# Values of four recurrent heads in one projection, and attention one head ahead, in a hybrid decoder layer

## The chip, the core and the metric

The kernel runs on one core of a Trainium2 chip, as one program. The core has a matrix engine (TensorE, "PE" in the profile, with its weight loads as "PEld"), a vector engine (VectorE, DVE), a scalar engine (ScalarE, ACT), a general engine (GpSimd, POOL) and an engine that here issues most transfers (SyncE, SP). Matrix products are accumulated in eight PSUM banks of 128 x 512 float32; everything else on the chip lies in SBUF. The metric is the device time of one execution in microseconds (us); lower is better. The median of 3 runs before the change is 2198.31 us (2196.97 to 2198.78).

## What is computed

One decoder layer over 2048 positions of width 1024, in float32. The part that the change touches is the mixer:

```python
u = rmsnorm(h, norm_mix_w[l])
proj = u @ w_in[l]                       # q, f, values, gate of 4 recurrent heads of 128; q, k, v of attention
f = lb + (1.0 - lb) * jax.nn.sigmoid(hf) # the decay of each key channel
# per head: S_t = diag(f_t) S_{t-1} + (1 - f_t) v_t^T,  o_t = S_t^T q_t   (in chunks)
o_hg = rmsnorm(o_hg, hg_norm_w[l]) * jax.nn.silu(hg)
# 8 query heads of 64 over 2 key heads, window of 128, a learned sink logit in each softmax
mix = jnp.concatenate([o_hg, o_att], axis=-1)
h = h + mix @ w_out[l]
```

After it come a gated MLP of width 2816 with a causal depthwise convolution, and a final rmsnorm. The change leaves those alone.

## The kernel before

The sequence is worked in two halves of 1024 positions, one after the other, and each half in three stages: the mixer, the output projection with the MLP's first two products (`out_proj`, `gate_up`), and the MLP's last product (`down`). A product in float32 is split: each operand is a high part and a low part, and three matmuls (high x high, high x low, low x high) stand for one. `prep` (L185) loads a weight block of 128 x 1024, lets ACT make the high part (L190) and DVE the low part (L191). `unit` (L194) is one projection to 128 output rows for 1024 positions: 8 blocks of the inner dimension x 3 x 2 halves = 48 matmuls of 512 columns, into two banks of the pool "mm", which has four.

The mixer runs over four recurrent heads, `h` = 0 to 3. `hgrn` is a Python generator, cut by `yield` into steps, and does for one head:

- projection f, then projection q ("hq" in the profile), then products of both (`Q` and `K`, one buffer each);
- a diagonal product ("pdiag", L544), then seven levels, m = 1, 2, 4, ... 64 (from L590 on). Each level is a matmul of `K` with `Q` ("plev", L569, L602 or L607), after which DVE multiplies `Q` (L609), `K` (L610) and `f` (L616), and the result is copied under a mask into the score matrix `ST`. The next level's matmul needs the new `Q` and `K`. In heads 0 to 2 levels below 32 take half as many matmuls, over a packed copy of `K` made by ACT (L566), with a small transfer to shift rows (L579). The last head takes 16 matmul instructions a level there (L602) and neither copy nor transfer;
- transposes of `K` ("pkn"), state updates ("pu", L647, then DVE L651), the gate's projection ("g"; in the last head it comes before the levels), the outputs ("po", L665 and L666, squared by ACT L667), their norm, transposes ("pot") and the gated result.

`attend` is a second generator, one call for two query heads (a "pair", `j` = 0 to 3): a projection ("q", scaled by DVE L435), scores ("psc", L459) with softmax on DVE and ACT, then in two steps transposes ("ppt"), masks (L498) and outputs ("poT", L506). Its banks are the two of the pool "at". In the last pair (`j` = 3) the outputs are split into high and low parts straight from the bank (L516, L517).

The loop over heads (from L1195 on) draws the steps of both generators in turn; pair `h` is drawn in head `h`. `project_v` (L688) makes the values of two heads at a time, in head 0 and in head 2: 8 blocks of positions x 8 x 3 = 192 matmuls of 256 columns, from two weight blocks in the ring "hi"/"lo", which has two of each. The bank is scaled into the values by ACT (L702), two copies of 128 x 128 each time.

The order in which the loop draws the steps is not the order on the engines. A planner simulates the program when it is built and fixes each engine's queue: what comes earlier in the program goes first, but work that waits is overtaken by later work that is ready, so far as its buffers are free. So a later unit's matmuls fill the time in which a level waits for DVE.

In the last head the mixed rows are split for the output projection (`split`, L223 and L224) into the buffers of `X`, which come free as the gate's projection has read them. `out_proj` then works in the order of blocks 0, 4, 1, 5, 2, 6, 7, 3, where block `h` is recurrent head `h` and block 4 + `j` is pair `j`. Its first three units ("pop") can begin before the mixer has ended. The table `BEHIND` holds the second one behind the first level of the last head, and parts of the third one behind "pu", "po" and "pot".

The pool "m" has eight buffers of 128 x 1024 for what lives across heads: each recurrent head's q and gate, each pair's q and output, and before the mixer the rows of x (first half) or of h (second half).

Of the kernel before, what the change touches and what calls it, by code (L numbers as in the profile page):

```python
# [8 lines left out]
F32 = mybir.dt.float32  # L9
# [30 lines left out]
NEG = -1.0e30  # L40
UT = 7
RAW = 3
VB = 2
KB = 2
WARM = 12
TAIL_WARM = 7
# [4 lines left out]
def hymba_layer(ctx: ExitStack, tc: tile.TileContext, a: dict, out: bass.AP):  # L51
# [378 lines left out]
    def attend(hf, j, X, invb, KS, V, mix, p):  # L430

        o = unit(a["w_att"][j], X, "q")
        qT = slot(f"att{j}")
        for b, bs in halves():
            nc.vector.scalar_tensor_tensor(qT[:, bs], o[b], 0.125, invb[:, bs], op0=ALU.mult, op1=ALU.mult)  # L435
            nc.scalar.activation(qT[:, bs], qT[:, bs], AF.Identity, bias=C.bq[:, j:j + 1])
        yield
        scs = []
        for g in range(NB):
            sc = p.tile([P, 2, 4, P], F32, tag="sc", name="sc", bufs=2)  # L440
            gs = slice(g * 512, (g + 1) * 512)
            for kv in range(2):
                r, other = rows(kv), rows(1 - kv)

                qh, ql = [p.tile([P, 512], F32R, tag="pp", name=n, bufs=4) for n in ("qh", "ql")]
                nc.scalar.copy(qh[r], qT[r, gs])
                nc.scalar.copy(qh[other], qT[r, gs])
                nc.vector.tensor_tensor(ql[r], qT[r, gs], qh[r].bitcast(F32), op=ALU.subtract)
                nc.scalar.copy(ql[other], ql[r].bitcast(F32))
                for i0 in (0, 2):  # L450
                    pb = ps("at", "psc")
                    first = hf == 0 and g == 0 and i0 == 0
                    for i in range(2):
                        n = g * 4 + i0 + i
                        w0 = 1 if first and i == 0 else 0
                        o = pb[:, i * 256 + w0 * P:(i + 1) * 256]
                        ks = slice((n + w0) * P, (n + 2) * P)
                        for t, qx in enumerate((qh, ql)):
                            nc.tensor.matmul(o, qx[:, (i0 + i) * P:(i0 + i + 1) * P], KS[:, kv, ks],  # L459
                                             start=t == 0, stop=t == 1)  # L460
                    pv = pb.rearrange("p (i w k) -> p i w k", i=2, w=2)
                    dst = sc[:, kv, i0:i0 + 2]
                    if first:
                        nc.vector.memset(dst[:, 0], NEG)
                        nc.scalar.copy(dst[:, 1], pv[:, 1, 0])
                    else:
                        nc.scalar.copy(dst, pv[:, :, 0])
                    nc.vector.copy_predicated(
                        dst, C.own.bitcast(U32).unsqueeze(1).to_broadcast([P, 2, P]), pv[:, :, 1])
            m = p.tile([P, 2, 4], F32, tag="mx", name="m", bufs=2)  # L470
            nc.vector.tensor_reduce(m.rearrange("p a b -> p (a b)"),
                                    sc.rearrange("p a b c -> p (a b) c"), axis=AX.X, op=ALU.max)
            sk = C.sinkb[:, j].unsqueeze(2).to_broadcast([P, 2, 4])
            nc.vector.tensor_tensor(m, m, sk, op=ALU.max)
            es = p.tile([P, 2, 4], F32, tag="es", name="es", bufs=2)
            nc.vector.tensor_tensor(es, sk, m, op=ALU.subtract)
            nc.vector.tensor_scalar(m, m, -1.0, None, op0=ALU.mult)
            den = p.tile([P, 2, 4], F32, tag="den", name="den", bufs=2)
            for kv in range(2):
                for i in range(4):  # L480
                    nc.scalar.activation(sc[:, kv, i], sc[:, kv, i], AF.Exp, bias=m[:, kv, i:i + 1],
                                         accum_out=den[:, kv, i:i + 1])
            nc.scalar.activation(es, es, AF.Exp)
            nc.vector.tensor_tensor(den, den, es, op=ALU.add)
            nc.vector.reciprocal(den, den)
            nc.vector.tensor_tensor(sc, sc, den.unsqueeze(3).to_broadcast([P, 2, 4, P]), op=ALU.mult)
            scs.append(sc)
        yield
        for g, sc in enumerate(scs):
            pm = []  # L490
            for kv in range(2):
                pm.append([p.tile([P, 4, P], F32, tag="pp", name=n, bufs=4) for n in ("po", "pp")])
                pt = ps("at", "ppt")
                for i in range(4):
                    nc.tensor.transpose(pt[:, i * P:(i + 1) * P], sc[:, kv, i], ident)
                ptv = pt.rearrange("p (i q) -> p i q", i=4)
                for dst, mk in zip(pm[kv], (C.ownT, C.prevT)):
                    nc.vector.tensor_tensor(dst, ptv, mk.unsqueeze(1).to_broadcast([P, 4, P]), op=ALU.mult)  # L498
            oT = ps("at", "poT")
            for i in range(4):  # L500
                n = g * 4 + i
                noprev = hf == 0 and n == 0
                for prev in range(1 if noprev else 2):
                    for kv in range(2):
                        r = rows(kv)
                        nc.tensor.matmul(oT[r, i * P:(i + 1) * P], V[:, n + 1 - prev, r], pm[kv][prev][:, i],  # L506
                                         start=prev == 0, stop=noprev or prev == 1)
            gs = slice(g * 512, (g + 1) * 512)
            if j < ATT_J - 1:
                nc.scalar.copy(qT[:, gs], oT)  # L510
                mix[4 + j] = qT
            else:
                if g == 0:
                    mix[4 + j] = new_x()
                h, l = mix[4 + j]
                nc.scalar.copy(h[:, gs], oT)  # L516
                nc.vector.tensor_tensor(l[:, gs], oT, h[:, gs].bitcast(F32), op=ALU.subtract)  # L517
            yield

    def hgrn(hf, h, X, invb, vs, WG, mix, p, fu=None):  # L520
# [166 lines left out]

    def project_v(hf, parts, X, rs, p):  # L688

        v = [p.tile([P, TT, P], F32, tag="v", name="v", bufs=VB) for _ in range(2)]  # L690
        for tt in range(TT):
            o = ps("mm", "pvv")
            t = slice(tt * P, (tt + 1) * P)
            for kt in range(KT):
                hi, lo = parts[kt // 4]
                xh, xl = X[kt]
                c = slice((kt % 4) * 256, (kt % 4 + 1) * 256)
                nc.tensor.matmul(o[:, 0:256], xh[:, t], hi[:, c], start=kt == 0, stop=False)  # L698
                nc.tensor.matmul(o[:, 0:256], xl[:, t], hi[:, c], start=False, stop=False)  # L699
                nc.tensor.matmul(o[:, 0:256], xh[:, t], lo[:, c], start=False, stop=kt == KT - 1)  # L700
            for i in range(2):
                nc.scalar.activation(v[i][:, tt], o[:, i * P:(i + 1) * P], AF.Identity, scale=rs[:, tt:tt + 1])  # L702
        return v

    def split_into(h, l, src, eng=None):
        return (nc.scalar.copy(h, src),  # L706
# [480 lines left out]
    for hf in range(NH):  # L1187
        X, kv, invb, rs, f0 = nxt
        with ExitStack() as st:
# [2 lines left out]
            mix = [None] * KT  # L1192
            vs = []
            M, WG = {}, {}
            for h in range(HG):  # L1195
                hg = hgrn(hf, h, X, invb, vs, WG, mix, p, f0 if h == 0 else None)
                at = attend(hf, h, X, invb, KS, V, mix, p)
                with tc.issue_after(summed.ins) if hf + h == 0 else ExitStack():
                    next(hg)
                if h == HG - 1:  # L1200
                    next(at)
                    next(hg)
                    for kt in (0, 4, 1, 5, 2, 6):
                        M[kt] = split(mix[kt])
                    next(hg)
                elif h % 2 == 0:
                    next(at)
                    wv = [prep(a["w_v"][h // 2, s]) for s in range(2)]
                    next(hg)
                    vs += project_v(hf, wv, X, rs, p)  # L1210
                else:
                    next(hg)
                    next(at)
                if h < HG - 1:
                    WG[h] = prep(a["w_g"][h])
                next(at)
                next(hg)
                if h < HG - 1:
                    next(hg)
                next(at)  # L1220
                if h < HG - 1:
                    next(at)
                    next(hg)
                else:
                    next(hg)
                    next(at)
            M[7], M[3] = mix[7], mix[3]
        with ExitStack() as st:
            p = pool(f"ffn{hf}", stack=st, reuse_waits="tile")
            kept, ops, hs, first, last = out_proj(hf, M, p)  # L1230
# [4 lines left out]
def _layout(i):  # L1235
# [14 lines left out]
    rows = [ar(P) + h * P for h in range(4)]  # L1250
    rows += [512 + np.concatenate([j * HD + ar(HD), (j + 4) * HD + ar(HD)]) for j in range(4)]
    w_out = i["w_out"][0][np.concatenate(rows)]
    w_v = np.stack([cols(w_in, 1024 + pr * 256 + ar(256)).reshape(P, 2, D).transpose(1, 0, 2) for pr in range(2)])
    conv = np.concatenate([i["conv_w"][0], i["conv_b"]], 0)
    d = {
        "xT": x.T.reshape(KT, P, S),
# [37 lines left out]
```

## Time and profile before

| What | Value |
|---|---|
| Time, median of 3 runs | 2198.31 us (2196.97 to 2198.78) |
| The profiled execution: span, first to last instruction | 2198.0 us |
| Mean granted TensorE clock | 0.997 |
| PE busy | 2180.4 us, 99% |
| DVE busy | 1639.5 us, 75% |
| ACT busy | 1049.9 us, 48% |
| Moved by DMA | 257.91 MB |
| Mixer, first half | about 45 to 400 us |
| Mixer, second half | about 1125 to 1490 us |

Matmuls overlap: a matmul of 512 columns is shown with some 390 ns, but the next one starts earlier, so "busy" is not a count of work done. The time from one matmul's start to the next one's is what a matmul costs in a row of them. The chain of waits shows that: there a piece is a run of instructions, with its start, the time that it took on the chain, and their count. In the lists of groups and of instructions the brackets at the end give the idle time of the engine ahead, and what ended it. The profile gives the span; the time that lies around it is not shown apart, and the median of the runs is 0.3 us above the span.

### The profile page before, as it was taken

How to read it: one execution, taken by the hardware profiler on the slowest of the kernel's cores; microseconds unless marked ns; L12 is line 12 of the kernel's file. 1: busy time of each engine (PE TensorE's matmuls, PEld its weight loads, DVE VectorE, ACT ScalarE, POOL GpSimd, SP SyncE). 2: the span in 40 equal slices, each digit the busy share in tenths (PEclk: the TensorE clock that was granted, in tenths of full speed). 3: DMA queues.
4: the chain of work that ended last, by engine and by line, in shares of the span. 5: the costliest groups of instructions: out<-in, count | busy, mean ns of one | idle time of the engine just before them, and what ended most of it. 6: DMA issues, size and time to landing. Idle time of an engine off the chain costs nothing.

```text
span 2198.0 us, 29524 instructions
## 1 busy us (share of the span) xinstructions
PE 2180.4 (99%) x11424; PEld 1834.0 (83%) x11424; DVE 1639.5 (75%) x2451; ACT 1049.9 (48%) x1848; POOL 6.3 (0%) x28
## 2 busy tenths in 40 slices
PE   9999999999999999999999999999999999999998
PEld 7988988888888888888889889888888888888888
DVE  6567568688887888885855666677888878887766
ACT  6445544454444445335735455544644444443353
POOL 1000000000000000000000000000000000000000
PEclk9999999999999999999999999999999999999999
DMA  4101112323333234964631111114132323259643
GB/s 155 51 32 48 39 41 68 119 74 102 104 109 108 89 127 143 372 241 156 209 125 41 44 36 51 58 39 134 58 125 92 125 91 109 98 183 393 233 144 130
DMA packets 94358, 257.91 MB, mean 117 GB/s; under 512 B 11594, under 2 KB 17546, under 8 KB 94218
## 3 DMA queue, kind: packets, MB, share of 16 engines
q1 hardware_dynamic: 88992, 251.30, 33.9%
q10 hardware_dynamic: 5226, 4.73, 0.7%
q8 instruction: 89, 1.46, 0.3%
q14 instruction: 51, 0.42, 0.1%
HBM read 195.10 MB, written 57.15 MB: 115 GB/s over the span
## 4 chain that ended last, share of the span: by engine, by line
PE 95%; DVE 3%; ACT 1%; DMA 1%; issue 0%; SPq 0%; DVEq 0%; ACTq 0%
PE X L877 7%; PE X L878 7%; PE X L879 7%; PE pop L212 7%; PE hq L212 4%; PE q L212 4%; PE f L212 4%; PE g L212 4%; PE Y L879 4%; PE Y L878 4%; PE Y L877 4%; PE pdx L1088 3%; PE pdx L1089 3%; PE pdx L1090 3%; PE pdy L1089 3%; PE pdy L1088 3%
## 5 line engine op out<-in xcount | busy, mean ns | idle before, releaser
L706 ACT CAST whi<-raw 128x1024 fp32r<-128x1024 f32 x88 | 92.6, 1053 | 109.2 <-PE X L878 68.2
L877 PE MATMUL X<-T,whi 128*128 128x512 f32 x352 | 136.9, 389 | 0.0
L878 PE MATMUL X<-T,whi 128*128 128x512 f32 x352 | 136.9, 389 | 0.0
L879 PE MATMUL X<-T,wlo 128*128 128x512 f32 x352 | 136.9, 389 | 0.0
L972 DVE SCALAR_TENSOR_TENSOR y<-ga,cw,y 128x1024 f32<-128x1024 f32 x88 | 112.5, 1281 | 26.0 <-ACT y L970 26.0
L884 ACT COPY u<-X 128x512 f32<-128x512 f32 x88 | 51.4, 585 | 133.3 <-PE X L879 133.1
L707 DVE TENSOR_TENSOR wlo<-raw,whi 128x1024 fp32r<-128x1024 f32 x88 | 107.3, 1220 | 0.0
L190 ACT CAST whi<-raw 128x1024 fp32r<-128x1024 f32 x57 | 59.5, 1048 | 93.1 <-PE q L212 31.9
L707 DVE TENSOR_TENSOR xld<-raw,xhd 128x1024 fp32r<-128x1024 f32 x72 | 80.8, 1133 | 19.1 <-ACT xhd L706 18.9
L706 ACT CAST xhd<-raw 128x1024 fp32r<-128x1024 f32 x72 | 69.7, 978 | 43.6 <-DMA raw<-act0T 14.8
L212 PE MATMUL pop<-XL,whi 128*128 128x512 f32 x256 | 86.1, 396 | 2.1 <-DVE XL L224 2.1
L212 PE MATMUL pop<-XH,wlo 128*128 128x512 f32 x256 | 85.2, 393 | 0.8 <-DVE wlo L191 0.8
L212 PE MATMUL pop<-XH,whi 128*128 128x512 f32 x256 | 84.5, 397 | 0.2
L878 PEld LDWEIGHTS X<-T,whi 128*128 128x128 f32 x352 | 66.1, 188 | 13.7
L877 PEld LDWEIGHTS X<-T,whi 128*128 128x128 f32 x352 | 66.1, 188 | 13.7
L879 PEld LDWEIGHTS X<-T,wlo 128*128 128x128 f32 x352 | 66.1, 188 | 13.7
L1088 PE MATMUL pdx<-xhd,hid 128*128 128x512 f32 x192 | 74.4, 391 | 1.0 <-ACT hid L706 1.0
L1089 PE MATMUL pdx<-xld,hid 128*128 128x512 f32 x192 | 74.7, 389 | 0.0
L1090 PE MATMUL pdx<-xhd,lod 128*128 128x512 f32 x192 | 73.7, 389 | 0.0
L698 PE MATMUL pvv<-whi,XH 128*128 128x256 f32 x256 | 73.5, 288 | 0.0
L191 DVE TENSOR_TENSOR wlo<-raw,whi 128x1024 fp32r<-128x1024 f32 x57 | 69.5, 1222 | 4.2 <-ACT whi L190 4.1
L699 PE MATMUL pvv<-whi,XL 128*128 128x256 f32 x256 | 72.6, 284 | 0.0
(379 smaller groups left out, 6563.3 us busy)
## 6 DMA issues: line engine op xcount, KB each, us to landing
wr<-in_w_down SPq DMA_DIRECT2D x90, 512.0 KB, 4.8
raw<-in_w_gate SPq DMA_DIRECT2D x44, 512.0 KB, 3.6
raw<-in_w_up SPq DMA_DIRECT2D x44, 512.0 KB, 3.6
raw<-act0T SPq DMA_DIRECT2D x20, 512.0 KB, 6.1
raw<-act1T SPq DMA_DIRECT2D x20, 512.0 KB, 10.1
act0B<-y SPq DMA_DIRECT2D x33, 256.0 KB, 2.6
act1B<-y SPq DMA_DIRECT2D x33, 256.0 KB, 2.4
raw<-in_w_out SPq DMA_DIRECT2D x16, 512.0 KB, 4.7
```

What stands on the lines that cost most here:

```text
L212: marks["unit"] = nc.tensor.matmul(o[b], w, x[:, bs], start=f, stop=l)
L698: nc.tensor.matmul(o[:, 0:256], xh[:, t], hi[:, c], start=kt == 0, stop=False)
L699: nc.tensor.matmul(o[:, 0:256], xl[:, t], hi[:, c], start=False, stop=False)
L706: return (nc.scalar.copy(h, src), (eng or nc.vector).tensor_tensor(l, src, h.bitcast(F32), op=ALU.subtract))
L707: (eng or nc.vector).tensor_tensor(l, src, h.bitcast(F32), op=ALU.subtract))
L877: nc.tensor.matmul(o, wh[:, ws], xh, start=i == 0 and not more, stop=False, skip_group_check=more)
L878: nc.tensor.matmul(o, wh[:, ws], xl, start=False, stop=False, skip_group_check=more)
L879: r = nc.tensor.matmul(o, wl[:, ws], xh, start=False, stop=i == 3, skip_group_check=more)
L972: nc.vector.scalar_tensor_tensor(y, g[:, w:w + HALF], C.cw[:, ft, w:w + 1], y, op0=ALU.mult, op1=ALU.add)
L1088: nc.tensor.matmul(o, wh[:, i, c], ah[:, i, cols], start=f, stop=False, skip_group_check=more)
L1089: nc.tensor.matmul(o, wh[:, i, c], al[:, i, cols], start=False, stop=False, skip_group_check=more)
L1090: nc.tensor.matmul(o, wl[:, i, c], ah[:, i, cols], start=False, stop=l, skip_group_check=more)
```

## The change

`project_v` is called once, in head 0, for all four heads. It takes four weight blocks (each for two of the eight inner blocks), two of them in the ring and two in the pool "m", and issues matmuls of 512 columns. Its bank is scaled by one ACT instruction of 128 x 512 into one tile for the values of all heads. The pool for values of two heads at a time goes.

The generators of all four pairs are made ahead of the loop. Head 0 draws pair 0 and pair 1, head 1 draws pair 2 (its projection after the levels, in the program's order), head 2 draws pair 3, and head 3 none. In head 3 seven blocks are split ahead of the levels, where there were six; the last pair's outputs are copied like the others' and split later. The host lays the weights out in four blocks of four heads. The scratch that the build sets aside for descriptors of another kind of DMA is made smaller.

```diff
-            if j < ATT_J - 1:
-                nc.scalar.copy(qT[:, gs], oT)
-                mix[4 + j] = qT
-            else:
-                if g == 0:
-                    mix[4 + j] = new_x()
-                h, l = mix[4 + j]
-                nc.scalar.copy(h[:, gs], oT)
-                nc.vector.tensor_tensor(l[:, gs], oT, h[:, gs].bitcast(F32), op=ALU.subtract)
+            nc.scalar.copy(qT[:, gs], oT)
+            mix[4 + j] = qT
...
-        v = [p.tile([P, TT, P], F32, tag="v", name="v", bufs=VB) for _ in range(2)]
+        v = p.tile([P, HG, TT, P], F32, name="v")
...
-                hi, lo = parts[kt // 4]
+                hi, lo = parts[kt // 2]
                 xh, xl = X[kt]
-                c = slice((kt % 4) * 256, (kt % 4 + 1) * 256)
-                nc.tensor.matmul(o[:, 0:256], xh[:, t], hi[:, c], start=kt == 0, stop=False)
-                nc.tensor.matmul(o[:, 0:256], xl[:, t], hi[:, c], start=False, stop=False)
-                nc.tensor.matmul(o[:, 0:256], xh[:, t], lo[:, c], start=False, stop=kt == KT - 1)
-            for i in range(2):
-                nc.scalar.activation(v[i][:, tt], o[:, i * P:(i + 1) * P], AF.Identity, scale=rs[:, tt:tt + 1])
-        return v
+                c = slice((kt % 2) * 512, (kt % 2 + 1) * 512)
+                nc.tensor.matmul(o, xh[:, t], hi[:, c], start=kt == 0, stop=False)
+                nc.tensor.matmul(o, xl[:, t], hi[:, c], start=False, stop=False)
+                nc.tensor.matmul(o, xh[:, t], lo[:, c], start=False, stop=kt == KT - 1)
+            nc.scalar.activation(v[:, :, tt], o.rearrange("p (h d) -> p h d", h=HG), AF.Identity,
+                                 scale=rs[:, tt:tt + 1])
+        return [v[:, h] for h in range(HG)]
...
+            at = [attend(hf, j, X, invb, KS, V, mix, p) for j in range(ATT_J)]
             for h in range(HG):
                 hg = hgrn(hf, h, X, invb, vs, WG, mix, p, f0 if h == 0 else None)
-                at = attend(hf, h, X, invb, KS, V, mix, p)
                 with tc.issue_after(summed.ins) if hf + h == 0 else ExitStack():
                     next(hg)
                 if h == HG - 1:
-                    next(at)
                     next(hg)
-                    for kt in (0, 4, 1, 5, 2, 6):
+                    for kt in (0, 4, 1, 5, 2, 6, 7):
                         M[kt] = split(mix[kt])
-                    next(hg)
-                elif h % 2 == 0:
-                    next(at)
-                    wv = [prep(a["w_v"][h // 2, s]) for s in range(2)]
-                    next(hg)
-                    vs += project_v(hf, wv, X, rs, p)
-                else:
-                    next(hg)
-                    next(at)
-                if h < HG - 1:
-                    WG[h] = prep(a["w_g"][h])
-                next(at)
+                    for _ in range(3):
+                        next(hg)
+                    break
+                own = at[h + 1] if h else at[0]
+                if h != 1:
+                    next(own)
+                if h == 0:
+                    wv = [prep(a["w_v"][s], s > 1) for s in range(4)]
+                next(hg)
+                if h == 1:
+                    next(own)
+                if h == 0:
+                    vs += project_v(hf, wv, X, rs, p)
+                WG[h] = prep(a["w_g"][h])
+                next(own)
+                if h == 0:
+                    next(at[1])
                 next(hg)
-                if h < HG - 1:
-                    next(hg)
-                next(at)
-                if h < HG - 1:
-                    next(at)
-                    next(hg)
-                else:
-                    next(hg)
-                    next(at)
-            M[7], M[3] = mix[7], mix[3]
+                next(hg)
+                next(own)
+                next(own)
+                if h == 0:
+                    next(at[1])
+                next(hg)
+                if h == 0:
+                    next(at[1])
+                    next(at[1])
+            M[3] = mix[3]
```

More of the change, by code (lines that the diff above doesn't have):

```diff
@@ L42 @@
 RAW = 3
-VB = 2
 KB = 2
@@ L1252, in _layout @@
     w_out = i["w_out"][0][np.concatenate(rows)]
-    w_v = np.stack([cols(w_in, 1024 + pr * 256 + ar(256)).reshape(P, 2, D).transpose(1, 0, 2) for pr in range(2)])
+    w_v = cols(w_in, 1024 + ar(512)).reshape(P, 4, D).transpose(1, 0, 2)
     conv = np.concatenate([i["conv_w"][0], i["conv_b"]], 0)
@@ L1285 @@
     arrays = {f"in_{k}": v for k, v in _layout({k: np.asarray(v) for k, v in inputs.items()}).items()}
-    nc = bacc.Bacc("TRN2", target_bir_lowering=False, num_devices=1)
+    nc = bacc.Bacc("TRN2", target_bir_lowering=False, num_devices=1, dynamic_dma_scratch_size=256)
     aps = {k[3:]: nc.dram_tensor(k, v.shape, mybir.dt.from_np(v.dtype), kind="ExternalInput").ap()
```

## The prediction, made before the changed kernel was run

> **What bounds the kernel now.** I read the page first, then the stretches of time head by head, then PE's waits and the chain of waits through one mixer. The page gives the bound:
>
> ```profile
> span 2198.0 us, 29524 instructions
> PE 2180.4 (99%) x11424; PEld 1834.0 (83%) x11424; DVE 1639.5 (75%) x2451; ACT 1049.9 (48%) x1848; POOL 6.3 (0%) x28
> ```
>
> PE is never long without a matmul, so a change is worth what it takes from PE's queue or adds to PE's waits. The next rows are stretches of the first half's mixer, cut at the diagonal products, so one row a head; columns are PE, weight loads, DVE, ACT, POOL busy, the granted clock and DMA.
>
> ```profile
> 68.00:155.00 87.00, 87.00 (x635) 77.75 (x634) 57.21 (x112) 46.30 (x119) 0.00 (x0) 1.00 0.14 42
> 155.00:248.00 93.00, 93.00 (x644) 82.16 (x643) 57.77 (x115) 46.67 (x119) 0.00 (x0) 1.00 0.13 38
> 248.00:342.00 94.00, 94.00 (x601) 80.38 (x601) 63.76 (x120) 52.51 (x121) 0.00 (x0) 1.00 0.20 63
> 342.00:400.00 58.00, 55.84 (x407) 47.27 (x406) 45.41 (x92) 21.53 (x72) 0.00 (x0) 0.97 0.09 28
> ```
>
> Heads 0 to 2 leave PE no idle time. The last head does (58.00 - 55.84 = 2.2 us), and there DVE is the fullest of the four rows (45.4 of 58). PE's own waits in 330 to 410 us and in 1420 to 1500 us, the two last heads, are these:
>
> ```profile
> PE pop L212 <- DVE XL L224: 0.7, 1, 0.7
> PE plev L602 <- DVE K L610: 0.7, 1, 0.7
> PE pdiag L544 <- DVE hg L680: 0.3, 1, 0.3
> ...
> PE pop L212 <- DVE XL L224: 1.4, 1, 1.4
> PE pop L212 <- DVE wlo L191: 0.4, 1, 0.4
> ```
>
> What the mixer's PE work costs is read from the chain of waits (start, time on the chain, what, count):
>
> ```profile
> 406.67 52.89 PE pop L212 x232
> 1147.40 10.88 PE q L212 x48
> 242.21 0.12 PE pvv L700
> 242.33 0.12 PE pvv L698
> 221.36 1.89 PE poT L506 x30
> ```
>
> A 512-column matmul in a row costs 10.88 / 48 = 0.2267 us (the long row gives 0.228), a 256-column one 0.12 us.
>
> **The change part by part.** *Values.* Each of the four calls has 192 matmuls of 256 columns; the page confirms the count for one of three lines:
>
> ```profile
> L698 PE MATMUL pvv<-whi,XH 128*128 128x256 f32 x256 | 73.5, 288 | 0.0
> ```
>
> So 768 x 0.12 = 92.2 us go and 384 x 0.2267 = 87.0 us come: -5.1 us. It lies on the path, since PE is the bound in head 0. Weight bytes are the same. Four blocks are cast ahead where two were, but those in the pool "m" need no ring buffer, and the ring's two come free half a position block (12 matmuls, 2.7 us) before the projection ends, which covers one ACT cast and one DVE subtraction (1.05 + 1.22 us by the groups below) of the gate's weights. If that cover fails, some 2 us a half are lost, and scores of pair 0 lie ready. SP issues four loads in a row ahead of the gate's; at a DMA share of 0.14 and 3.5 us a load they are hidden. In the second half the pool "m" is held by h until its rows are written out, and the last eight stores are issued at 1119 us, 39 us ahead of the first diagonal product; I cost that at nothing. ACT saves (64 x 0.365 against 16 x 0.58, the price of another copy of 128 x 512 from a bank) some 14 us that PE does not wait for. The smaller DMA scratch: nothing, the kernel's transfers use hardware queues alone.
>
> ```profile
> L190 ACT CAST whi<-raw 128x1024 fp32r<-128x1024 f32 x57 | 59.5, 1048 | 93.1 <-PE q L212 31.9
> L191 DVE TENSOR_TENSOR wlo<-raw,whi 128x1024 fp32r<-128x1024 f32 x57 | 69.5, 1222 | 4.2 <-ACT whi L190 4.1
> L702 ACT ACTIVATE v<-pvv,y 128x128 f32<-128x128 f32 x64 | 20.1, 365 | 40.8 <-PE pvv L700 36.5 <-DMA odd<-moved 1.5 <-PE po L665 1.4
> L424 ACT COPY V<-pv 128x512 f32<-128x512 f32 x4 | 2.3, 581 | 1.8 <-PE pv L423 1.8
> 1119.04 4.54 SPq L1183 DMA_DIRECT2D out<-h  x8
> raw<-in_w_v SPq DMA_DIRECT2D x8, 512.0 KB, 3.5
> ```
>
> [...]
>
> *The last head without attention.* The waits for XL, K and pdiag above come from DVE doing softmax and splits between the level's products; with them go 0.7 + 0.7 + 0.3 us in the first half and 1.4 us in the second. After that 1.4 us the clock fell too:
>
> ```profile
> 1439.70:1443.10 3.40, 3.26 (x8) 2.58 (x9) 3.40 (x8) 0.00 (x0) 0.00 (x0) 0.55 0.65 152
> 1439.84 1.06 PE L212 MATMUL pop<-XL,whi 128*128 128x512 f32 x2 [1.39 <-DVE XL L224]
> ```
>
> Eight matmuls took 3.4 us instead of 8 x 0.2267 = 1.8: 1.6 us more. Together -4.7 us for both halves. [...]
>
> But pair 3 also filled PE's time in the last head. One pair there is 62 outputs (about 3.8 us by the row of 30), 16 transposes (four take about 0.5) and 32 scores (0.12 each), some 9.5 us without its projection. What the levels have for cover is seen here, from the first "pop" to the fourth level:
>
> ```profile
> 334.41 1.61 PE pop L212 x7
> ...
> 346.72 1.90 PE L602 MATMUL plev<-Q,K 128*128 128x64 f32 x16
> ...
> 352.44 4.11 PE pop L212 x18
> 356.55 1.75 PE plev L602 x16
> 358.31 0.69 DVE Q L609
> 359.01 0.60 DVE K L610
> ...
> 367.72 3.63 PE poT L506 x28
> 371.35 0.76 PE ppt L495 x4
> 372.11 1.73 PE plev L602 x16
> ```
>
> A level's hand-off to DVE and back is Q and K, 0.69 + 0.60 = about 1.35 us with the steps between. From level 4 on, outputs and transposes of pair 3 filled it. After the change there is the second "pop" unit (42 of its 48 matmuls, 9.5 us), which the planner spends about 18 at a time (4.1 us), so on two hand-offs; block 7, now early, gives 12 matmuls (2.7 us) for one more. Four of seven stay open: 4 x 1.35 = 5.4 us a half, +10.8 us. Bounds: 0, if the first unit is still there too; 7 x 1.35 x 2 = +18.9, if nothing is. I take the middle, as before the first unit was all but played out (it starts at 334.4 us) when the levels began at 346.7. One fall of the clock in each half, as the one above: +3.2 (0 to 6.4).
>
> *Heads 1 and 2.* Before, 93 and 94 us passed there from diagonal to diagonal. PE's own work in such a head becomes four units (43.5), a pair (9.5), the head's small products and some changes of form, about 72 us, as the second call of `project_v` (192 x 0.12 = 23) has moved to head 0. Of the small products I estimate 15 us: five levels at 0.89, two at about 1, diagonal and state products about 2 each, two sets of transposes, 16 pairs of output matmuls at 0.22. The head's chain has to shrink as much. It can, since in the last head the same steps after the levels took far less when nothing lay between (first row: a level of head 0):
>
> ```profile
> 82.08 0.89 PE plev L569 x8
> ...
> 381.65 0.64 PE pkn L640 x4
> 382.32 0.59 ACT Kn L641
> 382.95 2.05 PE pu L647 x16
> ...
> 388.31 0.38 ACT on L667 x2
> 388.73 0.49 PE po L665 x2
> ```
>
> There the open hand-offs cost 0.7 us and some 0.3 us three times. If half of that falls open in heads 1 and 2: +0.8 a head and half less what is hidden, I take +2 for all four. Bounds: 0, and 4 heads x 8 us where the chain does not shrink below 80 us: +32. DVE would be at 58 of 72 us, 80%, near the last head's 78%, which left PE 2.2 us idle; hence near the lower end.
>
> *The split of pair 3* as a whole block: one cast and one subtraction of 1024 columns for two of 512 each; the same, and earlier.
>
> **Sum.** -5.1 - 4.7 + 10.8 + 3.2 + 2 = +6.2 us on 2198.0 for this execution, whose span is 0.3 us under the median: 2204.4, say 2204.
>
> **The rivals.** *The gain comes through (faster).* At the last head's first level the first "pop" unit's 42 matmuls are still unplayed, so that all seven hand-offs are covered (4.1 us each is wanted for a planner, but 1.35 would do: 84 matmuls are 19 us, 14 hand-offs). Then the new terms vanish: 2198.3 - 5.1 - 4.7 = 2188. For it: DVE's load in that head falls by pair 3's products, so the chain needs less cover. Against: the unit was played out before. The point where it decides is some 30 unplayed matmuls at the first level.
>
> *Heads 1 and 2 bound by their chain.* All the filling stands in head 0, where the chain does not need it, and heads 1 and 2 take 80 us against 72 of work. Half of the +32 above, +16 more: 2220. For it: 93 and 94 us before. Against: no wait of PE before 330 us.
>
> *Nothing moves.* The cover in the last head is short by two hand-offs a half, which with one fall of the clock eats the gain: -9.8 + 4 x 1.35 + 3.2 = -1.2: 2197.
>
> **How the numbers follow.** The forecast gets 0.38, faster 0.35, the chain-bound one 0.12, nothing 0.15. A measurement of this kernel tells 0.2%, 4.4 us, from no change: faster is below 2193.9, slower above 2202.7. The forecast's own range is 2199 to 2212 (open hand-offs from two to six), so 0.04 of it counts as no change; faster 0.35, same 0.18, slower 0.47. The range of 8 in 10 goes from 2184 (the faster case less some 4 us of changes of form that go with the interleaving) to 2220.
>
> **What would show it.** Right: 384 "pvv" matmuls at 0.227 us; in the last head idle time of PE before "plev" that DVE's K or Q ends, some 5 us a half, and a clock below 1.0 there; no wait for XL of pair 3. Wrong: no idle time at "plev" (then faster), or idle time before "plev", "pu" and "po" in heads 1 and 2 (then slower than 2212); or a wait for weights at the end of the values.

## The result and the profile after

The changed kernel takes 2236.62 us (median of 4 runs, 2235.96 to 2237.74) against 2198.55 us of the kernel before beside it: 1.0177 times as long, interval 1.0162 to 1.0191, some 38 us more. The profiled execution's span is 2234.9 us, 36.9 us above that of before. The two lines of the page that answer to the first fence of the prediction:

```profile
span 2234.9 us, 28743 instructions
PE 2190.5 (98%) x11040; PEld 1828.7 (82%) x11040; DVE 1639.7 (73%) x2449; ACT 1039.4 (47%) x1798; POOL 6.0 (0%) x28
```

PE has 384 instructions fewer and is busy for longer. The loss is all in the two mixers: the long row of "pop" matmuls behind the first one starts at 427.45 us (406.67 before), that behind the second one at 1533.52 us (1496.74 before), so 20.8 us are lost in the first and 16.0 in the second. The next rows are the changed kernel's stretches, cut at the diagonal products (columns as in the prediction): the four heads of the first half, then heads 2 and 3 of the second half.

```profile
68.00:188.00 120.00, 120.00 (x696) 101.03 (x695) 65.42 (x124) 56.81 (x129) 0.00 (x0) 1.00 0.14 43
188.00:297.00 109.00, 109.00 (x706) 92.28 (x706) 73.45 (x151) 58.75 (x159) 0.00 (x0) 1.00 0.13 39
297.00:361.00 64.00, 53.62 (x380) 46.14 (x379) 51.68 (x103) 33.67 (x88) 0.00 (x0) 0.95 0.21 60
361.00:421.00 60.00, 52.52 (x315) 46.37 (x314) 32.35 (x63) 10.81 (x28) 0.00 (x0) 0.83 0.09 27
...
1400.00:1468.00 68.00, 62.52 (x426) 52.48 (x425) 54.41 (x108) 37.21 (x95) 0.00 (x0) 0.97 0.20 62
1468.00:1527.00 59.00, 51.52 (x312) 45.74 (x313) 31.78 (x62) 10.81 (x28) 0.00 (x0) 0.83 0.09 27
```

Head 0 grew from 87 to 120 us and head 1 from 93 to 109, both with PE full. Heads 2 and 3 have little left to do (head 2: 64 us for 94), and in that time PE stands idle: 10.4 and 7.5 us in the first half, 5.5 and 7.5 in the second. The last head takes about as long as before (60 us for 58), with three quarters of the matmuls, and its clock is 0.83. PE's waits in 60 to 430 us and in 1165 to 1535 us name what is late:

```profile
PE pot L671 <- DVE on L666: 4.2, 1, 4.2
PE psc L458 <- DVE sc L467: 3.3, 1, 3.3
PE plev L594 <- DVE K L602: 3.0, 2, 1.5
PE plev L599 <- DVE K L602: 2.4, 2, 1.5
PE pkn L632 <- DVE F L612: 1.9, 1, 1.9
PE plev L599 <- DVE f L608: 1.5, 1, 1.5
PE pkn L632 <- DVE K L602: 1.5, 1, 1.5
...
PE pot L671 <- DVE on L666: 4.2, 1, 4.2
PE plev L594 <- DVE K L602: 3.0, 2, 1.5
PE plev L599 <- DVE K L602: 1.5, 1, 1.5
PE plev L599 <- DVE f L608: 1.5, 1, 1.5
PE pkn L632 <- DVE K L602: 1.5, 1, 1.5
```

Of these, L594 and the 1.5 us waits at L599 and at "pkn" are the last head's levels; "pot", "psc", the wait for F and the 0.9 us that are left of the first half's L599 stand in head 2. In the second half head 2 waits at "pot" and 1.2 us for the gate's input ("g"). Before, all the waits of a mixer came to 2.3 us. The chain of waits through the last head shows two more things:

```profile
368.72 6.90 PE pop L211 x30
375.62 1.73 PE plev L594 x16
377.35 5.09 PE pop L211 x22
382.44 1.74 PE plev L594 x16
384.21 0.69 DVE Q L601
384.90 0.61 DVE K L602
...
385.65 1.98 PE plev L594 x16
387.65 0.69 DVE Q L601
388.35 0.61 DVE K L602
389.10 3.66 PE plev L594 x16
...
402.12 3.66 PE pu L639 x16
```

The second "pop" unit goes in two pieces, 30 and 22 matmuls with the rest of the first unit, into the hand-offs of levels 1 and 2; from level 4 on each hand-off is open. And the same 16 matmuls that take 1.73 us at one level take 3.66 us two levels on: the clock has fallen to half (granted clock 1.00 from 387.0 to 388.6 us, 0.50 from 388.64 to 405.71).

### The profile page after: what moved, and what is told of

Its sections match the earlier page's. It is cut to its first block, busy times and chain, and to the rows that moved or that the text cites. A ratio compares the mean times of both kernels' runs of the same rounds, so it can differ in the third digit from the quotient of the medians.

```text
span 2234.9 us, 28743 instructions
## 1 busy us (share of the span) xinstructions
PE 2190.5 (98%) x11040; PEld 1828.7 (82%) x11040; DVE 1639.7 (73%) x2449; ACT 1039.4 (47%) x1798; POOL 6.0 (0%) x28
## 3 DMA queue, kind: packets, MB, share of 16 engines
q1 hardware_dynamic: 88992, 251.30, 33.4%
## 4 chain that ended last, share of the span: by engine, by line
PE 94%; DVE 4%; ACT 1%; issue 1%; DMA 1%; SPq 0%; ACTq 0%; DVEq 0%
PE pop L211 7%; PE X L869 7%; PE X L870 7%; PE X L871 7%; PE q L211 4%; PE f L211 4%; PE pdx L1080 4%; PE Y L871 4%; PE pdx L1082 4%; PE Y L869 4%; PE Y L870 4%; PE pdx L1081 4%; PE g L211 4%; PE hq L211 3%; PE pdy L1081 3%; PE pdy L1080 3%
## 5 line engine op out<-in xcount | busy, mean ns | idle before, releaser
L601 DVE TENSOR_TENSOR Q<-Q,f 128x512 f32<-128x512 f32 x56 | 38.6, 690 | 81.7 <-PE plev L599 31.5
L869 PE MATMUL X<-T,Sh 128*128 128x512 f32 x176 | 68.7, 390 | 1.5 <-ACT s L876 1.5
```

What stands on the lines that cost most here:

```text
L869: nc.tensor.matmul(o, wh[:, ws], xh, start=i == 0 and not more, stop=False, skip_group_check=more)
```

## The experiments

Twelve kernels were run, each timed beside the kernel before. Two theories stood at the start. *Late chain*: the filling for PE (values of heads 2 and 3, a pair) that moved into head 0 delays the chain of levels and states of heads 1 to 3, which then runs bare at the end. *Bare last head*: all of the loss is that the last head lost its pair. The results together:

| Kernel | Median, us | Ratio to before, interval |
|---|---|---|
| changed kernel | 2236.62 | 1.0177, 1.0162 to 1.0191 |
| e1, values alone | 2236.97 | 1.0176, 1.0158 to 1.0194 |
| e2, attention alone | 2219.61 | 1.0095, 1.0079 to 1.0111 |
| e3, pair 1 in head 1 | 2237.04 | 1.0174, 1.0158 to 1.0190 |
| e4, pair 3 in the last head | 2242.79 | 1.0200, 1.0184 to 1.0216 |
| e5, values in head 0, 256 columns | 2238.47 | 1.0181, 1.0166 to 1.0197 |
| e6, second unit shared out | 2213.54 | 1.0068, 1.0053 to 1.0083 |
| e7, matmuls nobody reads | 2236.27 | 1.0175, 1.0158 to 1.0192 |
| e8, before, second unit shared out | 2196.14 | 0.9990, 0.9981 to 0.9999 |
| e9, e2 and the sharing-out | 2195.87 | 0.9989, 0.9979 to 0.9998 |
| e10, e7 with half as many | 2224.78 | 1.0122, 1.0106 to 1.0138 |
| e11, e6 and the first unit held back | 2210.15 | 1.0053, 1.0035 to 1.0071 |
| e12, e1 and the sharing-out | 2216.05 | 1.0083, 1.0067 to 1.0099 |

### One half of the change at a time (e1, e2)

e1 is the kernel before with the new `project_v`, its four weight blocks and their layout:

```diff
                 elif h % 2 == 0:
                     next(at)
-                    wv = [prep(a["w_v"][h // 2, s]) for s in range(2)]
+                    if h == 0:
+                        wv = [prep(a["w_v"][s], s > 1) for s in range(4)]
                     next(hg)
-                    vs += project_v(hf, wv, X, rs, p)
+                    if h == 0:
+                        vs += project_v(hf, wv, X, rs, p)
```

> The kernel before with the values of all four heads made in head 0 in 512-column matmuls, attention as before (pair h in head h). Late chain (the loss is filling moved into head 0, where the chain of heads 1 to 3 cannot use it): part of the loss comes already, since 23 us of values leave head 2, but pair 1 and pair 3 stay where they were; -5.1 us for the values and up to +10 us for heads 2 and 3: 2196 to 2204 us. Bare last head (the loss is only that the last head has no pair): the last head keeps pair 3, so the values' 5 us come through: 2193 us, and the last head's waits as before.

Measured: 2236.97 us. Moving the values alone loses all that the whole change loses, though every pair is where it was. Both theories missed the size: the late chain gave 2204 at most, and the bare last head, which gave 2193, is out as the only cause. The stretches of heads 2 and 3 in e1's first half:

```profile
277.00:359.00 82.00, 70.99 (x475) 60.56 (x475) 62.98 (x128) 46.39 (x123) 0.00 (x0) 0.94 0.20 60
359.00:416.00 57.00, 51.00 (x354) 44.61 (x351) 33.01 (x66) 11.43 (x30) 0.00 (x0) 0.88 0.06 20
```

Head 2 is left with 71.0 us of PE work where it had 94, and takes 82 us. The difference has the size of the values' call, but only some 6 us of it are values. The first two of the next rows are heads 1 and 2 of the kernel before, the matmuls of "pvv" alone; the other two are heads 1 and 2 of e1, the instructions on "f" alone, PE first in each row:

```profile
155.00:248.00 93.00, 18.96 (x147) 18.06 (x147) 3.32 (x11) 1.00 0.13 38
248.00:342.00 94.00, 6.11 (x47) 5.54 (x46) 1.79 (x6) 1.00 0.20 63
176.00:277.00 101.00, 23.44 (x96) 17.67 (x96) 16.10 (x26) 1.26 (x2) 1.00 0.13 39
277.00:359.00 82.00, 0.00 (x0) 0.00 (x0) 16.00 (x26) 1.15 (x2) 0.94 0.20 60
```

Before, most of the second call's values were played at the end of head 1, and each of the heads 1 and 2 played 48 matmuls of "f", the projection for the next head. With the values gone, PE took the next ready work there: e1's head 1 plays the projection f of the last head as well, and the gate of head 2 in the same way (96 matmuls of "g" for 48). Both are missing in head 2. The changed kernel does the same (96 matmuls of "f" in head 1 and one in head 2 in the first half, 65 and 31 in the second). What PE then waits for in e1's head 2 is above all the softmax and the masks of pair 3, and its own chain only for 1.1 us:

```profile
PE ppt L495 <- DVE y L176: 6.4, 1, 6.4
PE poT L506 <- DVE pp L498: 3.5, 1, 3.5
```

Pair 3, drawn in the last head, is no cover from the third level on: half of its transposes and outputs are played ahead of the levels, the rest by level 2, and four hand-offs are open all the same.

e2 is the other half, the changed kernel with the old `project_v`, called in heads 0 and 2:

```diff
-                if h == 0:
-                    wv = [prep(a["w_v"][s], s > 1) for s in range(4)]
+                if h % 2 == 0:
+                    wv = [prep(a["w_v"][h // 2, s]) for s in range(2)]
...
-                if h == 0:
+                if h % 2 == 0:
                     vs += project_v(hf, wv, X, rs, p)
```

> The changed kernel's order of the attention (two pairs in head 0, none in the last), but the values by pairs of heads in 256-column matmuls, in head 0 and in head 2, as before. Late chain: 23 us of values in head 2 come back as filling, so head 0 takes some 98 us and head 2 is covered; 2205 to 2215 us. Bare last head: the last head is as bare as in the changed kernel and the values' gain of 5 us is lost as well: 2240 us.

Measured: 2219.61 us, 17.0 us below the changed kernel although the narrow matmuls cost 5 us more. This lies 5 us above the late chain's range and 20 below the other's figure. With the values' call back, head 2 plays its own gate and the last head's f again (96 matmuls of "g" and 48 of "f"), and it is almost without waits (0.7 us); the last head is as bare as in the changed kernel:

```profile
268.00:351.00 83.00, 82.29 (x552) 70.73 (x550) 58.90 (x111) 41.93 (x104) 0.00 (x0) 1.00 0.21 66
351.00:410.00 59.00, 51.20 (x310) 44.91 (x311) 31.58 (x62) 10.71 (x28) 0.00 (x0) 0.83 0.09 27
```

So there are two losses, and they do not add up: the attention's order alone loses 21 us, the values alone 38, both together 38.

### Where the pairs stand (e3, e4)

e3 draws pair 1 in head 1 beside pair 2:

```diff
-                own = at[h + 1] if h else at[0]
+                own = at[(0, 1, 3)[h]]
...
-                if h == 0:
-                    next(at[1])
+                if h == 1:
+                    next(at[2])
```

> The changed kernel with pair 1 moved from head 0 to head 1 (head 0: pair 0 and all values; head 1: pairs 1 and 2; head 2: pair 3; head 3: none). Late chain: the second head's diagonal products come some 20 us earlier (about 168 us instead of 188 us in the first half), and half or more of the 38 us of loss is recovered: 2208 to 2220 us. Bare last head: the last head is as bare as before the move, its open hand-offs and its slow clock stay: 2233 to 2237 us.

Measured: 2237.04 us, no change. The late chain, as I had put it, failed here. Heads 1 and 2 did begin 12 and 13 us earlier, at 176 and 284 us for 188 and 297, but the last head only 3 us earlier (359 for 362). The first of these rows is head 1, with two pairs and PE full; the second is head 2:

```profile
176.00:284.00 108.00, 107.49 (x658) 91.78 (x657) 74.53 (x149) 64.24 (x164) 0.00 (x0) 1.00 0.14 42
284.00:359.00 75.00, 67.67 (x489) 57.67 (x488) 58.87 (x115) 41.88 (x103) 0.00 (x0) 0.95 0.16 51
```

Head 1 is as full and as long as before the move (108 us for 109). Head 2 has more to do (489 matmuls for 380), but it takes 75 us for 64 with 7.3 us of idle time, and gives most of the lead back. The long row behind the first mixer begins 4 us earlier than in the changed kernel (423.43 for 427.45), that behind the second one 2 us (1531.82 for 1533.52).

e4 draws pair 3 in the last head, with its outputs split straight from the bank as before, and no pair in head 2:

```diff
-                own = at[h + 1] if h else at[0]
+                own = (at[0], at[2], None)[h]
...
                 if h == HG - 1:
+                    next(at[3])
                     next(hg)
```

> The changed kernel with pair 3 back in the last head, handled there as in the kernel before (head 0: pairs 0 and 1; head 1: pair 2; head 2: none). Late chain: the last head is covered, but head 2 now has no filling at all and its levels open, at half clock in part; half of the loss at most is recovered: 2215 to 2230 us. Bare last head: the loss is gone and the values' gain stays: 2193 to 2200 us.

Measured: 2242.79 us, 6 us more than the changed kernel and above both expectations. A pair in the last head does not cure it once the values are gone from head 2; what it covers there is missing in head 2 (76 us, PE 67.6 us busy), and the rest comes open as in e1. The bare last head alone is out for good.

### Place or width of the values (e5)

In e1 the levels of head 0 come every 6 us, where they came every 4: a block of 24 wide matmuls takes 5.4 us (24 x 0.2267). e5 keeps the narrow matmuls and makes both calls in head 0 (and takes the smaller scratch of the changed kernel for the room):

```diff
                     next(hg)
-                    vs += project_v(hf, wv, X, rs, p)
+                    if h == 0:
+                        vs += project_v(hf, wv[0:2], X, rs, p)
+                        vs += project_v(hf, wv[2:4], X, rs, p)
```

> The kernel before with both calls for the values made in head 0 (256-column matmuls as before, two weight blocks in the ring and two in the pool m); attention as before. It has the place of the values of e1 without their width. If their place decides (23 us of filling leave head 2 for head 0), the loss of e1 is here too and the 5 us that the wide matmuls save are not: 2237 to 2245 us. If their width decides (a piece of 24 matmuls that takes 5.4 us fits a hand-off of 3 us badly, one of 2.9 us fits it well), head 0's levels keep their pace of 4 us and the time is 2198 to 2208 us.

Measured: 2238.47 us: the place decides. The levels kept their pace of 4 us up to level 64, and then the rest of the values stood in one piece ahead of the transposes of K (from 101 us to 123). In the program all the values stand ahead of head 0's state updates, and so, whatever their width, they are spent there. The time is only 1.5 us above e1's, although 768 narrow matmuls cost 5.2 us more by their starts than 384 wide ones (94.5 us in the kernel before, 89.3 in the changed kernel); where the other 3.7 us went was not traced.

### Sharing out what is left (e6, e8, e9, e12)

e6 takes the changed kernel and gives out the second unit one block a level, with marks set at levels 32 and 64 too:

```diff
-BEHIND = {1: {0: 1}, 2: {0: "pu", 2: "po", 5: "pot"}}
+BEHIND = {1: {0: 1, 1: 2, 2: 4, 3: 8, 4: 16, 5: 32, 6: 64}, 2: {0: "pu", 2: "po", 5: "pot"}}
```

> The changed kernel with the second unit of the output projection given out in the last head at one block (6 matmuls, 1.36 us) a level, where the first two levels took 30 and 22 matmuls and the other five nothing. If the open hand-offs of the last head (5 at 1.48 us a half) and the clock that falls through them carry a good part of the loss: 4 us of waits and 4 to 5 us of clock less in each half, 2218 to 2223 us. If the loss lies elsewhere, and the last head only shows it: 2233 to 2237 us.

Measured: 2213.54 us, 23 us of the 38 back, more than I had expected. The chain of waits in its last head, where six matmuls stand in each hand-off:

```profile
375.62 2.14 PE pop L211 x9
377.76 1.73 PE plev L594 x16
379.49 1.44 PE pop L211 x6
...
380.97 1.97 PE plev L594 x16
382.94 1.45 PE pop L211 x6
```

The same edit on three other kernels:

> The kernel before with the same sharing-out of the second unit as e6. There pair 3 covers the levels from the third on, so that there is next to nothing to gain: 2195 to 2202 us. A gain as large as that of e6 would mean that the sharing-out helps whatever the attention does.

> e2 (the changed kernel's order of the attention, values by pairs of heads as before) with the second unit given out one block a level, as in e6. If the loss of e2 is the bare last head (its five open hand-offs of 1.6 to 1.8 us a half with their clock) and nothing else, the sharing-out takes back what it took back in e6, 10 us a half at most: 2200 to 2206 us. If something else in e2 costs its 21 us (two pairs in head 0, one pair late in head 1): 2212 to 2220 us.

> e1 (values of all heads in head 0 in 512-column matmuls, attention as before) with the second unit given out one block a level. If moving the values alone lays the same levels of the last head bare as the whole change does (late chain), the sharing-out takes back much of it here too, though pair 3 is in the last head: 2212 to 2222 us. If the loss of e1 lies ahead of the last head: 2230 to 2237 us.

Measured: e8 2196.14 us, e9 2195.87, e12 2216.05. On the kernel before it gains some 2 us, since pair 3 covers most of its levels. On e1 it gains 21 us, so e1 and the changed kernel lose most of it in the same place. On e2 it gains 23.7 us, more than either expectation allowed, and takes the whole loss away. In e9's last head PE is full and its clock whole:

```profile
351.00:397.00 46.00, 45.02 (x308) 37.90 (x309) 31.51 (x63) 10.60 (x28) 0.00 (x0) 1.00 0.11 35
```

Here the two steps do add up: values back in head 2 17.0 us, sharing-out 23.1, both 40.7. Thus the changed order of the attention costs nothing if the second unit is shared out, and the new place of the values costs the rest. e9, with the attention one head ahead, and e8 are both a little faster than the kernel before; their intervals end at 0.9998 and 0.9999, so that this is at the edge of what can be told, and they can't be told apart.

### The price of the clock (e7, e10)

e7 puts matmuls that nobody reads (128 x 128, float32) into the open hand-offs of the changed kernel, e10 half as many:

```diff
+            if h == HG - 1 and m >= 4:
+                without_use(ps("at", "idle"), 5, marks[m])
...
+        if h == HG - 2:
+            without_use(ps("at", "idle"), 13, marks["po"])
```

> The changed kernel with matmuls that nobody reads (128 x 128, float32) behind each level of the last head from the third on (10 each) and behind the outputs of head 2 (30). The waits stay as long as they are; only the clock can differ. If the half clock after the open hand-offs costs what the windows say (7 us a half between the outputs of head 2 and the state updates of the last head): 2222 to 2227 us. If the clock is no cost of its own: 2236 us or some more.

> e7 with half as many matmuls that nobody reads: 5 a level and 13 behind the outputs of head 2, 1.15 and 3.0 us by the 2.29 us that 10 took in e7, where the hand-offs are 1.48 and 4.2 us. In e7 they were too many by 0.8 us a level and 2.5 us in head 2, which is as much as the clock gave back. If the half clock is a cost of its own, some 7 us a half: 2222 to 2227 us. If not: 2234 to 2238 us.

Measured: e7 2236.27 us, e10 2224.78. By its time alone e7 would say that the clock is no cost of its own; its trace says otherwise. In e7 the clock was whole in the last head (1.00 from 361 to 421 us, where the changed kernel has 0.83), but ten of these matmuls (20 records) take 2.29 us, in a hand-off of 1.48, and the thirty 6.70 us, where the wait had been 4.2:

```profile
356.85 6.70 PE idle L93 x60
...
386.54 2.29 PE idle L93 x20
```

That filling was too large and gave the gain back. In e10 it fits. The changed kernel's and then e10's stretch of the last head from level 4 to the state updates (20 us):

```profile
383.00:403.00 20.00, 12.62 (x103) 11.70 (x103) 9.15 (x18) 2.48 (x5) 0.00 (x0) 0.64 0.00 1
```

```profile
383.00:403.00 20.00, 18.45 (x175) 16.77 (x175) 11.94 (x26) 2.38 (x5) 0.00 (x0) 1.00 0.01 2
```

The hand-offs stay as long as they were. Only the matmuls between them are faster, for instance the 16 of "pu" 2.05 us where they took 3.66:

```profile
398.21 2.05 PE pu L641 x16
```

So the half clock is a cost of its own: 11.8 us of the 38, some 6 in each half.

### The open end of head 2 (e11)

e11 is e6 with two blocks of the first unit held back until head 2's outputs, and the order of the blocks changed so that the held ones are ready by then:

```diff
-BEHIND = {1: {0: 1, 1: 2, 2: 4, 3: 8, 4: 16, 5: 32, 6: 64}, 2: {0: "pu", 2: "po", 5: "pot"}}
+BEHIND = {0: {4: "po2"}, 1: {0: 1, 1: 2, 2: 4, 3: 8, 4: 16, 5: 32, 6: 64}, 2: {0: "pu", 2: "po", 5: "pot"}}
...
-        order = [0, 4, 1, 5, 2, 6, 7, 3]
+        order = [0, 4, 1, 5, 6, 7, 2, 3]
```

> e6 with two blocks (12 matmuls, 2.7 us) of the first unit of the output projection held back until the outputs of head 2 are issued; the blocks' order is 0, 4, 1, 5, 6, 7, 2, 3, so that the two held blocks are ready there. In e6 PE waits there 4.2 us for the normalised outputs and then runs at half clock. If the open end of head 2 is the rest of the loss: 2.7 us of wait and 1 us of clock less in each half, 2204 to 2209 us. If what is held back is missed where it was taken from: 2212 to 2216 us.

Measured: 2210.15 us, 3.4 us below e6, between the two expectations, and the intervals of the two overlap, so this is inconclusive as to size. Its waits tell where the filling was taken from. "pot" fell from 4.2 us to 1.4 in both halves; in the first half "pkn", which had no wait for K in head 2 in e6, now waits:

```profile
PE psc L458 <- DVE sc L467: 3.3, 1, 3.3
PE pkn L632 <- DVE K L602: 2.9, 1, 2.9
PE plev L599 <- DVE K L602: 2.1, 1, 2.1
PE pot L673 <- DVE on L668: 1.4, 1, 1.4
```

What remains to the kernel before, 11.5 us, and the 5 us of the wide matmuls on top, were not traced further run by run; e9, which differs from e6 only in the values, has only 0.5 us of these waits in a mixer, at "pot".

### What follows

Both first theories fell in the form that I gave them: putting a pair elsewhere recovers nothing (e3, e4), and the last head is not the only bare one (e1). What the runs support is this. PE plays whatever is ready, and more of it at a hand-off than the hand-off needs (30 and 22 matmuls, 6.90 and 5.09 us, in the changed kernel's last head, for hand-offs of 1.48); work that is moved to an early head lets the work behind it move up too. When the filling has run out, the rest of the chain runs bare and half-clocked. The kernel before had 23 us of filling in each half that came late, the second call of `project_v`: the program's order kept it behind head 0, and it was played at the end of head 1 and in head 2, so that head 2's gate and the last head's f were still there for head 2's levels. Shown are the two prices, for both halves together: 17 us for the values' call in head 2, with the 5 us of narrow matmuls already taken off, and 23 us for the sharing-out. So the 46 us of matmuls in that call (both halves) were worth about half their own length. Why the place of a pair does not matter was not shown; e3's rows show that head 1 stays as long and that head 2 grows, and no run held a pair back.

## Why the prediction was wrong

The direction was right, the size was not: 2204 us with a range up to 2220, against 2236.6. By its own steps, both halves together:

- *Values, -5.1 us.* Right. The 384 wide matmuls take 89.3 us from start to start, against 94.5 for the 768 narrow ones: -5.2 us. PE does not wait for weights at their end (the first half's trace shows no wait of PE from 110 to 135 us), and "pvv" has no wait at all.
- *The last head's waits that go, -4.7 us.* PE no longer waits for XL of pair 3, as predicted. This was a saving on top of which larger waits came.
- *Open hand-offs of the last head, +10.8 us.* Right in kind and nearly in size. I had four of 1.35 us open in each half; there are five of 1.48 (the fifth at "pkn"), 14.8 us. The second unit was spent on two hand-offs, as I had said, but in pieces of 30 and 22, not 18. As idle time, the last heads have 15.0 us where they had 4.1 (from the stretches; before, the second half's was 55.04 us busy of 57.00), +10.9 where my terms gave about +7.7 without the clock.
- *One fall of the clock a half, +3.2 us (0 to 6.4).* Mis-sized. I priced a fall by the one that I had seen before, 1.6 us, and overlooked another in the first half: the 28 "poT" matmuls that take 3.63 us in the prediction's own chain, where 30 take 1.89, ran at half clock (granted clock 0.50 from 368.26 to 371.67 us). So a fall in each half was there already. In the changed kernel the clock stays at half from the second open hand-off of the last head to its state updates (0.50 from 388.64 to 405.71 us), and falls at the end of head 2 as well (0.50 from 357.92 to 364.75 us); e10, whose mean clock is that of before (0.997), prices that at 11.8 us.
- *Heads 1 and 2, +2 us.* This is the step that failed, first in the work and then in the wait. I gave each of these heads four units and a pair, about 72 us, and bounded its chain at 80; then I let the chain shrink to the work, because PE waited nowhere before, and took a value near the lower end. But the matmuls do not stay in the head that draws them. The prediction's own line with a "pvv" at 242.21 us, ahead of head 2's diagonal product at 248, shows the second call's values in head 1. With them gone, PE played the gate of head 2 and the last head's f in head 1 as far as they were ready. Head 1 is 109 us long and full, and head 2 is left with 53.6 us of work in 64 in the first half and 62.5 in 68 in the second. It is idle for 10.4 and 5.5 us, together 15.9 where I had +2. Of the waits in the first half, 7.0 us are on the head's own chain ("pot", F, K) and 3.3 on pair 3's softmax. That e1's head 2 has 71.0 us, close to my 72, is luck: its parts are others. The rival with heads 1 and 2 bound by their chain, 2220 us, had half of this mechanism, for head 2 alone, and I gave it 0.12.
- *Where the cover goes.* Moving the second call of `project_v` was priced by its own matmuls and by head 2's work. I should have asked what it had covered: by e1 moving it alone is worth the whole 38 us, though pair 3 stays in the last head there.

Together the measured terms are -5.2 + 15.9 + 10.9 + 11.8 = 33.4 us of 36.9 in the profiled executions. The rest, 3.5 us, was not traced; changes of form in the new interleaving, which the sum does not price, may be a part of it (the first "pvv" behind a level takes 0.43 us on the changed kernel's chain, at 107.47 and 114.44 us, where the next ones take 0.23). The signs that the prediction named did show it: idle time at "plev" ended by DVE in the last head with a clock below 1.0. As the mark of more than 2212 us I had named idle time before "plev", "pu" and "po" in heads 1 and 2; it came in head 2 alone, before "psc", "pkn", "pot" and, in the second half, "g", and before "plev" for 0.9 us only.

## What to carry to other kernels

Before work is drawn earlier in a kernel whose bound engine never waits, count what that work covers where it stands: cut the trace at the serial chain's steps, take the moved work away from the stretch, let the ready work behind it move up, and compare what is left with the length of the chain alone. Filling that can be played at any time is spent early and in pieces larger than the gaps; tie it to the steps that need it, as one block a level did here (23 us for a longer table and the marks that it needs). Price an open gap with the clock that it costs: nearly a third of this loss (11.8 of 38 us, by e10) was not idle time but matmuls at half speed behind it.

## What the runs showed of the hardware

In the last heads the clock of TensorE fell without a pause of PE of more than 1.5 us. In the changed kernel's last head PE waits 1.48 us, works 2 us, waits 1.48 us again, and 4.9 us after the first of these waits began (384.21 to 389.10 in the chain) the same matmuls take 3.66 us for 1.98; the granted clock is 0.50 from 388.64 to 405.71 us. With five matmuls that nobody reads in each such hand-off (e10; PE busy for 18.45 us of the 20 from 383 to 403 us, where it was 12.62) the clock stays at 1.00. In the kernel before it fell after less: in the first half's last head the granted clock is 0.50 from 368.26 to 371.67 us, and PE's only wait between 355 and 380 us is one of 0.7 us; ahead of the fall stood levels of 64 columns and transposes. In the traces of the kernel before and of the changed kernel, each stretch at a clock of 0.50 but the one at the kernel's end lasts 3.41 us (three before; two in the changed kernel), 6.83 us (two in the changed kernel, at the end of head 2) or 17.07 us (two, in its last heads). What makes the clock fall was not tested.
